# A transformer block on one core: relu chunks transposed out of the banks, their transfers on one queue, relu and square in one instruction

## The chip, the cores and the metric

The kernel runs on one core of a Trainium2 chip. The core has five engines with a queue of instructions each: TensorE (PE, matmuls into the banks of PSUM), VectorE (DVE), ScalarE (ACT), GpSimd (POOL) and SyncE (SP); DMA transfers are issued from the queue of an engine and run on 16 DMA engines. Each queue runs in order, and engines wait for each other by semaphores. The metric is the device time of one execution in microseconds, a median over runs.

## The reference

One layer (DEPTH = 1) of a decoder trunk over 256 tokens of width 2048, in float32. A conditioning vector gives shifts, scales and gates; then come a token mixer and a channel mixer, each with a normalisation before and after. What the change touches is the channel mixer and the gates' rows:

```python
mod = (c_act @ w_ada[l] + b_ada[l]).reshape(b, N_MOD, 1, d)
shift1, scale1, gate1, shift2, scale2, gate2 = [mod[:, i] for i in range(N_MOD)]
h = rms_norm(x, norm_g[l, 0]) * (1.0 + scale1) + shift1
y = token_mixer(h, ...)                      # pooling, gMLP and sparse attention, gated and merged
x = x + gate1 * rms_norm(y, norm_g[l, 1])
h = rms_norm(x, norm_g[l, 2]) * (1.0 + scale2) + shift2
f = jnp.square(jax.nn.relu(h @ w_ff1[l])) @ w_ff2[l]       # 2048 -> 8192 -> 2048
x = x + gate2 * rms_norm(f, norm_g[l, 3])
```

## The kernel before, in words

Tokens are two tiles of 128 (NT = 2), the width 16 tiles of 128 channels (KT = 16). Every large product goes through `gemm` (512 output columns, all 256 tokens): a weight tile of 128 x 2048 (four channel tiles, 1 MB) is loaded into one of three tiles named `raw`, and `split` turns half of it at a time into a hi part on ScalarE (`whi`, L175) and a lo part on VectorE (`wlo`, L176), in three buffers each. `mm_a` then makes three matmuls per channel tile and token tile (hi x hi, lo x hi, hi x lo; L188 to L190), so that a `gemm` is 8 splits and 96 matmuls. A split unit is 12 matmuls. The splits have a raised priority, and a scheduler that follows priorities sets the final order of each queue.

The feed-forward part runs in four passes (`qt`). A pass has four chunks (`m`) of 512 hidden columns: `gemm` of w_ff1, relu of the two banks on ScalarE (L953), and `to_channels`, which turns the chunk from tokens to channels on the partitions. VectorE transposes 32 x 32 blocks (L934), 16 DMAs of 32 KB each move the blocks to their partitions (`moved<-tr`, L938; eight from SyncE, eight from GpSimd), ScalarE squares (L942), and `hi_lo` makes the chunk's hi part (`fhi`, ScalarE, L396) and lo part (`flo`, VectorE, L397). Then four `gemm` of w_ff2 read the pass's 16 channel tiles of fhi and flo, the last chunk's tiles in the last two split units of the first of them.

Beside the products, `fill` steps side work once for every weight tile. In the feed-forward part it is `ada_gate`: 16 loads of 1 MB into `raw` tiles with a reduction each on VectorE (L263), which give the second gate as columns, and then `to_rows` (L290 to L299), which turns the gate's 16 columns to rows with a TensorE transpose, copies them to a `raw` tile, and sends them through DRAM to all partitions as `gg`. `to_rows` also runs once for the first gate, between the products of the token mixer. All loads of `raw` tiles go from SyncE's queue.

## Time and profile before

| | us |
|---|---|
| median of 3 runs (lowest, highest) | 1487.23 (1486.66, 1489.45) |
| the profiled execution, its own time | 1489.17 |
| its span, first to last instruction | 1487.4 |
| TensorE busy | 1417.6 (95%) |
| VectorE busy | 1049.2 (71%) |
| ScalarE busy | 813.1 (55%) |
| GpSimd busy | 94.6 (6%) |

The profile is of one execution. A busy time is the union of an engine's instructions; matmuls overlap each other, so that one which takes 0.39 us starts some 0.23 us after the one before. In the timelines, the bracket at the end of a row is how long the engine stood idle before it, and what ended that. The mean granted clock of TensorE over the span is 0.994 of full speed.

### The profile page before, as it was taken

How to read it: one execution, taken by the hardware profiler on the slowest of the kernel's cores; microseconds unless marked ns; L12 is line 12 of the kernel's file. 1: busy time of each engine (PE TensorE's matmuls, PEld its weight loads, DVE VectorE, ACT ScalarE, POOL GpSimd, SP SyncE). 2: the span in 40 equal slices, each digit the busy share in tenths (PEclk: the TensorE clock that was granted, in tenths of full speed). 3: DMA queues.
4: the chain of work that ended last, by engine and by line, in shares of the span. 5: the costliest groups of instructions: out<-in, count | busy, mean ns of one | idle time of the engine just before them, and what ended most of it. 6: DMA issues, size and time to landing. Idle time of an engine off the chain costs nothing.

```text
span 1487.4 us, 17515 instructions
## 1 busy us (share of the span) xinstructions
PE 1417.6 (95%) x6362; PEld 1155.3 (78%) x6362; DVE 1049.2 (71%) x1315; ACT 813.1 (55%) x1184; POOL 94.6 (6%) x165
## 2 busy tenths in 40 slices
PE   3989999899999999999999999999999999999997
PEld 2777787788777777778778888888887788887886
DVE  6988887668988886788786666566655555554555
ACT  4566666864677873444475543355434453344542
POOL 0000001002010010000001210022001120011100
PEclk9999999999999999999999999999999999999999
DMA  8989788657667568888855776677764765555653
GB/s 315 386 329 368 298 330 307 219 175 255 230 227 285 196 243 319 313 309 302 320 199 184 260 271 239 234 267 269 248 242 172 271 221 190 190 208 190 221 198 113
DMA packets 64695, 376.02 MB, mean 253 GB/s; under 512 B 10288, under 2 KB 14560, under 8 KB 24160
## 3 DMA queue, kind: packets, MB, share of 16 engines
q1 hardware_dynamic: 58848, 364.35, 67.9%
q0 software_dynamic: 5760, 10.55, 2.3%
q8 instruction: 50, 0.82, 0.2%
q14 instruction: 37, 0.30, 0.1%
HBM read 364.35 MB, written 2.11 MB: 246 GB/s over the span
## 4 chain that ended last, share of the span: by engine, by line
PE 79%; DVE 9%; DMA 6%; ACT 3%; issue 2%; SPq 0%; POOL 0%; DVEq 0%; ACTq 0%
PE ps_mm L189 25%; PE ps_mm L190 25%; PE ps_mm L188 24%; DVE wlo L176 4%; DMA raw<-in_w_adaT_dram 3%; DVE raw L263 2%; ACT whi L175 1%; DMA raw<-in_win_g_dram 1%; PE ps_x L666 1%; DMA x_h<-in_x_dram 1%; DMA raw<-in_w_br_nsa_dram 1%; PE ps_pv L658 1%; PE ps_pv L530 0%; DMA raw<-in_w_out_dram 0%; PE ps_pv L657 0%
## 5 line engine op out<-in xcount | busy, mean ns | idle before, releaser
L176 DVE TENSOR_TENSOR wlo<-raw,whi 128x1024 fp32r<-128x1024 f32 x479 | 571.9, 1205 | 321.0 <-ACT whi L175 319.5
L175 ACT ACTIVATE whi<-raw 128x1024 fp32r<-128x1024 f32 x479 | 492.5, 1035 | 493.5 <-PE ps_mm L190 391.3
L189 PE MATMUL ps_mm<-wlo,hhi 128*128 128x512 f32 x1240 | 491.3, 396 | 14.3 <-DVE wlo L176 14.3
L188 PE MATMUL ps_mm<-whi,hhi 128*128 128x512 f32 x1240 | 485.3, 395 | 11.3 <-ACT whi L175 7.6
L190 PE MATMUL ps_mm<-whi,hlo 128*128 128x512 f32 x1240 | 486.9, 393 | 0.0
L189 PEld LDWEIGHTS ps_mm<-wlo,hhi 128*128 128x128 f32 x1240 | 235.2, 190 | 72.1 <-DVE wlo L176 24.9
L188 PEld LDWEIGHTS ps_mm<-whi,hhi 128*128 128x128 f32 x1240 | 234.8, 190 | 62.5 <-ACT whi L175 10.3
L190 PEld LDWEIGHTS ps_mm<-whi,hlo 128*128 128x128 f32 x1240 | 234.5, 189 | 47.8 <-DVE hlo L316 0.4
L263 DVE CUSTOM_DVE_ANT_0 raw<-raw,sil 128x2048 f32<-128x2048 f32 x96 | 220.0, 2293 | 11.6 <-DMA raw<-in_w_adaT_dram 11.4
L189 PE MATMUL ps_mm<-wlo,fhi 128*128 128x512 f32 x496 | 193.2, 390 | 0.0
L188 PE MATMUL ps_mm<-whi,fhi 128*128 128x512 f32 x496 | 193.2, 390 | 0.0
L190 PE MATMUL ps_mm<-whi,flo 128*128 128x512 f32 x496 | 193.2, 390 | 0.0
L938 POOL DMA_DIRECT2D moved<-tr x128 | 62.6, 497 | 739.3 <-DVE tr L934 560.4
L190 PEld LDWEIGHTS ps_mm<-whi,flo 128*128 128x128 f32 x496 | 93.2, 188 | 19.3
L189 PEld LDWEIGHTS ps_mm<-wlo,fhi 128*128 128x128 f32 x496 | 93.2, 188 | 19.2
L188 PEld LDWEIGHTS ps_mm<-whi,fhi 128*128 128x128 f32 x496 | 93.2, 188 | 19.2
L397 DVE TENSOR_TENSOR flo<-r32c,fhi 128x512 fp32r<-128x512 f32 x32 | 20.7, 688 | 24.1 <-ACT fhi L396 24.1
L393 ACT ACTIVATE ps_mm<-part 128x512 f32<-128x512 f32 x40 | 23.5, 597 | 11.5 <-DVE part L382 7.0
L639 ACT ACTIVATE e<-e,m 128x128 f32<-128x128 f32 (+1 forms) x64 | 28.2, 443 | 0.7 <-DVE m L636 0.6
L942 ACT ACTIVATE r32c<-moved 128x512 f32<-128x512 f32 x32 | 18.4, 622 | 16.0 <-DMA moved<-tr 15.4
L953 ACT ACTIVATE r_t<-ps_mm 128x512 f32<-128x512 f32 x32 | 18.8, 588 | 14.7 <-PE ps_mm L190 14.7
L189 PE MATMUL ps_mm<-wlo,qe 128*128 128x512 f32 x64 | 25.3, 395 | 1.3 <-DVE wlo L176 1.3
(284 smaller groups left out, 1103.8 us busy)
## 6 DMA issues: line engine op xcount, KB each, us to landing
raw<-in_w_ff_dram SPq DMA_DIRECT2D x128, 1024.0 KB, 5.0
raw<-in_w_adaT_dram SPq DMA_DIRECT2D x96, 1024.0 KB, 6.2
raw<-in_win_g_dram SPq DMA_DIRECT2D x32, 1024.0 KB, 5.1
raw<-in_win_e_dram SPq DMA_DIRECT2D x24, 1024.0 KB, 5.3
raw<-in_win_e_dram SPq DMA_DIRECT2D x24, 768.0 KB, 6.3
raw<-in_w_out_dram SPq DMA_DIRECT2D x16, 1024.0 KB, 6.3
raw<-in_w_br_nsa_dram SPq DMA_DIRECT2D x8, 1024.0 KB, 5.2
raw<-in_win_e_dram SPq DMA_DIRECT2D x12, 512.0 KB, 6.0
```

The lines of the kernel that those rows point to most:

```text
L175: A.activation(hv, v, AF.Copy)
L176: V.tensor_sub(lv, v, hv.bitcast(F32))
L188: T.matmul(outs[t], ahi[:, kt, ts_], hv[:, k, c0:c0 + n], start=f, stop=False, skip_group_check=True)
L189: T.matmul(outs[t], ahi[:, kt, ts_], lv[:, k, c0:c0 + n], start=False, stop=False, skip_group_check=True)
L190: T.matmul(outs[t], alo[:, kt, ts_], hv[:, k, c0:c0 + n], start=False, stop=l, skip_group_check=True)
L263: V.tensor_tensor_reduce(raw, raw, sil, 0.5, 0.0, ALU.mult, ALU.add, accum_out=col)
L393: A.activation(ps, early[e][0][:, b * 512:(b + 1) * 512], AF.Copy)
L397: V.tensor_sub(lo, src, hi.bitcast(F32))
L639: A.activation(e[:, br, 0:L], e[:, br, 0:L], AF.Exp, scale=-1.0, bias=m8[:, hh, br:br + 1], accum_out=s8[:, hh, br:br + 1])
L938: (nc.sync if j % 2 else G).dma_start(moved[32 * j:32 * j + 32, q].rearrange("p t m i -> p (t m i)"), tr[32 * q:32 * q + 32, j].rearrange( ...
L942: A.activation(r32[:, :, t * P:(t + 1) * P].rearrange("p m (q i) -> p m q i", i=32), moved[:, :, t].rearrange("p q m i -> p m q i"), AF.Sq ...
L953: A.activation(r_t[:, t], ps[t], AF.Relu)
```

## The change

In `to_rows` the gate's rows are copied into the first 16 partitions of the constant tile's triangle (`triu`, last read by the gMLP mixer), and no `raw` tile is taken. In the feed-forward part the relu on ScalarE goes: VectorE transposes straight from the two banks, all 16 DMAs of a chunk are issued from GpSimd, and one VectorE instruction on the moved tile takes max(x, 0) * x in place. The hi and lo parts are then made by token tile (t) instead of by pairs of channel tiles, and read the moved tile in the order of the channels.

```diff
-        gr = st.tile([P, 2048], F32, name="raw", tag="raw", bufs=3)[0:KT, 0:P]
+        gr = triu[0:KT]
         V.tensor_copy(gr, tb[0:KT, 0:P])
         row = dp.tile([KT, P], F32, name="row", tag="row", bufs=2)
         G.dma_start(row, gr)
...
-    def to_channels(m, r_t):
+    def to_channels(m, ps):
         tr = fl.tile([P, 4, NT, 4, 32], F32, name="tr")
         for t in range(NT):
-            V.transpose(tr[:, :, t], r_t[:, t].rearrange("p (m j i) -> p j m i", m=4, j=4))
-        moved = fl.tile([P, 4, NT, 4, 32], F32, name="moved", tag="moved", bufs=1)
+            V.transpose(tr[:, :, t], ps[t].rearrange("p (m j i) -> p j m i", m=4, j=4))
+        moved = fl.tile([P, 4, NT, 4, 32], F32, name="moved")
         for q in range(4):
             for j in range(4):
-                (nc.sync if j % 2 else G).dma_start(moved[32 * j:32 * j + 32, q].rearrange("p t m i -> p (t m i)"),
-                                                    tr[32 * q:32 * q + 32, j].rearrange("p t m i -> p (t m i)"))
-        r32 = fl.tile([P, 4, S], F32, name="r32c", tag="r32c", bufs=1)
+                G.dma_start(moved[32 * j:32 * j + 32, q].rearrange("p t m i -> p (t m i)"),
+                            tr[32 * q:32 * q + 32, j].rearrange("p t m i -> p (t m i)"))
+        mf = moved.rearrange("p q t m i -> p (q t m i)")
+        V.scalar_tensor_tensor(mf, mf, 0.0, mf, ALU.max, ALU.mult)
         for t in range(NT):
-            A.activation(r32[:, :, t * P:(t + 1) * P].rearrange("p m (q i) -> p m q i", i=32),
-                         moved[:, :, t].rearrange("p q m i -> p m q i"), AF.Square)
-        for k in range(2):
-            s = slice(4 * m + 2 * k, 4 * m + 2 * k + 2)
-            hi_lo(flat(fhi[:, s]), flat(flo[:, s]), flat(r32[:, 2 * k:2 * k + 2]))
+            ts_ = slice(t * P, (t + 1) * P)
+            hv, lv = (f[:, 4 * m:4 * m + 4, ts_].rearrange("p m (q i) -> p m q i", i=32) for f in (fhi, flo))
+            hi_lo(hv, lv, moved[:, :, t].rearrange("p q m i -> p m q i"))
...
             ps = gemm(ff1_v, qt * 4 + m, act) if qt or m else ps_first
-            r_t = fl.tile([P, NT, 512], F32, name="r_t", tag="r_t", bufs=2)
-            for t in range(NT):
-                A.activation(r_t[:, t], ps[t], AF.Relu)
-            to_channels(m, r_t)
+            to_channels(m, ps)
```

The scheduler also puts other instructions in another order. VectorE's queue in the last pass, one chunk before the change (tr is the transposed chunk, wlo the lo part of a weight split, flo the chunk's lo part):

```order
L934 STREAM_TRANSPOSE tr<-r_t 128x4x128
L176 TENSOR_TENSOR wlo<-raw,whi 128x1024
L934 STREAM_TRANSPOSE tr<-r_t 128x4x128
L176 TENSOR_TENSOR wlo<-raw,whi 128x1024 x3
L397 TENSOR_TENSOR flo<-r32c,fhi 128x512 x2
L176 TENSOR_TENSOR wlo<-raw,whi 128x1024 x4
```

And the same chunk now:

```order
L934 STREAM_TRANSPOSE tr<-ps_mm 128x4x128 x2
L176 TENSOR_TENSOR wlo<-raw,whi 128x1024 x4
L941 SCALAR_TENSOR_TENSOR moved<-moved 128x1024
L176 TENSOR_TENSOR wlo<-raw,whi 128x1024
L397 TENSOR_TENSOR flo<-moved,fhi 128x4x128 x2
L176 TENSOR_TENSOR wlo<-raw,whi 128x1024 x3
```

The two transposes stand together, and the new instruction stands behind four lo parts, with one more between it and the chunk's own lo part.

ScalarE's queue before, at the first two chunks of the third pass (r_t is the relu's output, r32c the square's, fhi the chunk's hi part):

```order
L953 ACTIVATE r_t<-ps_mm 128x512
L175 ACTIVATE whi<-raw 128x1024
L953 ACTIVATE r_t<-ps_mm 128x512
L175 ACTIVATE whi<-raw 128x1024
L942 ACTIVATE r32c<-moved 128x4x128 x2
L396 ACTIVATE fhi<-r32c 128x512 x2
L175 ACTIVATE whi<-raw 128x1024 x6
L953 ACTIVATE r_t<-ps_mm 128x512
L175 ACTIVATE whi<-raw 128x1024
L953 ACTIVATE r_t<-ps_mm 128x512
L175 ACTIVATE whi<-raw 128x1024 x3
L942 ACTIVATE r32c<-moved 128x4x128 x2
```

And now, in the same place:

```order
L396 ACTIVATE fhi<-moved 128x4x128 x2
L175 ACTIVATE whi<-raw 128x1024 x8
L396 ACTIVATE fhi<-moved 128x4x128 x2
L175 ACTIVATE whi<-raw 128x1024 x8
L396 ACTIVATE fhi<-moved 128x4x128 x2
```

Relus and squares are gone, and eight hi parts of weights stand between the hi parts of one chunk and the next.

SyncE's queue before at the first gate's rows, in the token mixer (adaT are the loads of the side work, x_ the tile of the residual):

```order
L843 DMA x_5631<-in_x_dram 128x2048
L165 DMA raw<-in_w_br_nsa_dram 128x2048
L262 DMA raw<-in_w_adaT_dram 128x2048
L843 DMA x_5631<-in_x_dram 128x2048
L165 DMA raw<-in_w_br_nsa_dram 128x2048
L262 DMA raw<-in_w_adaT_dram 128x2048
L165 DMA raw<-in_w_br_nsa_dram 128x2048
L262 DMA raw<-in_w_adaT_dram 128x2048
L165 DMA raw<-in_win_g_dram 128x2048 x2
```

And now:

```order
L843 DMA x_5630<-in_x_dram 128x2048
L165 DMA raw<-in_w_br_nsa_dram 128x2048
L262 DMA raw<-in_w_adaT_dram 128x2048
L165 DMA raw<-in_w_br_nsa_dram 128x2048
L262 DMA raw<-in_w_adaT_dram 128x2048
L165 DMA raw<-in_w_br_nsa_dram 128x2048
L262 DMA raw<-in_w_adaT_dram 128x2048
L843 DMA x_5630<-in_x_dram 128x2048
L165 DMA raw<-in_win_g_dram 128x2048 x2
```

The second load of x stands four loads later than before, behind the loads that surround the gate's rows. In the feed-forward part SyncE's queue keeps the loads alone.

## Rows read from the trace of the kernel before

**Rows 1.** The page, busy time of each engine.
```profile
PE 1417.6 (95%) x6362; PEld 1155.3 (78%) x6362; DVE 1049.2 (71%) x1315; ACT 813.1 (55%) x1184; POOL 94.6 (6%) x165
```
**Rows 2.** Stretches: length, busy time (instructions) by engine, clock, DMA share, GB/s.
```profile
785.00:1150.00 365.00, 365.00 (x1612) 302.48 (x1611) 225.94 (x219) 168.46 (x185) 35.19 (x72) 1.00 0.69 241
...
1050.00:1100.00 50.00, 50.00 (x222) 41.43 (x221) 31.06 (x29) 19.12 (x19) 0.00 (x0) 1.00 0.68 242
1150.00:1200.00 50.00, 46.70 (x193) 37.61 (x192) 26.11 (x26) 25.07 (x30) 8.89 (x18) 0.93 0.72 252
...
1350.00:1400.00 50.00, 47.68 (x203) 38.77 (x202) 25.92 (x25) 23.63 (x30) 9.78 (x20) 0.97 0.59 194
```
**Rows 3.** Timeline of TensorE at 1155 us: start, duration, instruction, idle before.
```profile
1155.00 1.22 PE L188 MATMUL ps_mm<-whi,hhi 128*128 128x512 f32 x2 [3.27 <-ACT whi L175]
...
1157.28 0.63 PE L189 MATMUL ps_mm<-wlo,hhi 128*128 128x512 f32 x1
```
**Rows 4.** The chain that ended last, at 1143 to 1149 us.
```profile
1143.75 0.51 SPq L938
...
1148.81 4.98 DMA raw<-in_w_ff_dram
```
**Rows 5.** Waits of SyncE's queue: total us, times, longest us.
```profile
SPq L938 <- DVE tr L934: 45.2, 16, 13.6
...
SPq L165 <- DMA row<-raw: 12.7, 2, 6.6
```
**Rows 6.** Timeline of ScalarE at both stalls.
```profile
1150.40 1.15 ACT L942 ACTIVATE r32c<-moved 128x512 f32<-128x512 f32 x2 [5.84 <-DMA moved<-tr]
1151.59 1.15 ACT L396 ACTIVATE fhi<-r32c 128x512 fp32r<-128x512 f32 x2
1153.89 2.00 ACT L175 ACTIVATE whi<-raw 128x1024 fp32r<-128x1024 f32 x2 [1.16 <-DMA raw<-in_w_ff_dram]
...
1358.07 1.15 ACT L942 ACTIVATE r32c<-moved 128x512 f32<-128x512 f32 x2 [5.29 <-DMA moved<-tr]
```
**Rows 7.** Timeline of GpSimd, an undisturbed chunk and the one of 1347 us.
```profile
1194.46 3.90 POOL L938 DMA_DIRECT2D moved<-tr  x8 [17.83 <-DVE tr L934]
...
1351.46 1.96 POOL L938 DMA_DIRECT2D moved<-tr  x4 [2.72 <-issue]
```
**Rows 8.** Timeline of VectorE in the undisturbed chunk.
```profile
1191.18 0.71 DVE L934 STREAM_TRANSPOSE tr<-r_t 128x512 f32<-128x512 f32 x1 [0.35 <-ACT r_t L953]
...
1195.04 1.23 DVE L176 TENSOR_TENSOR wlo<-raw,whi 128x1024 fp32r<-128x1024 f32 x1 [0.87 <-ACT whi L175]
...
1200.48 1.23 DVE L176 TENSOR_TENSOR wlo<-raw,whi 128x1024 fp32r<-128x1024 f32 x1 [1.49 <-ACT whi L175]
```
**Rows 9.** Timeline of ScalarE in the undisturbed chunk.
```profile
1190.55 0.60 ACT L953 ACTIVATE r_t<-ps_mm 128x512 f32<-128x512 f32 x1 [0.98 <-PE ps_mm L190]
1191.23 1.06 ACT L175 ACTIVATE whi<-raw 128x1024 fp32r<-128x1024 f32 x1
```
**Rows 10.** Transfers to moved: chunk of 1194 us, chunk of 1347, chunks to 1100.
```profile
DMA to landing us min/median/max: 1.7/1.8/2.2
...
DMA to landing us min/median/max: 1.7/1.9/4.9
...
DMA to landing us min/median/max: 1.8/3.4/5.0
```
**Rows 11.** Two lines of VectorE: durations ns min/median/max, first and last start, forms.
```profile
L142 DVE SCALAR_TENSOR_TENSOR sil<-xnT,sil x2: 1225/1226/1226, 5.8 to 7.3; 128x1024 f32<-128x1024 f32 x2
...
L966 DVE COPY fsum<-ps_mm x8: 680/682/684, 879.2 to 945.1; 128x512 f32<-128x512 f32 x8
```
**Rows 12.** The first gate's rows: SyncE, TensorE, and the stretch around.
```profile
585.92 0.33 SPq L165 DMA_DIRECT2D raw<-in_w_br_nsa_dram  x1
...
584.68 1.38 PE L343 MATMUL ps_x<-cst,mab 128*128 128x128 f32 x8 [1.55 <-DVE mab L815]
...
575.00:600.00 25.00, 21.49 (x95) 16.21 (x93) 17.48 (x22) 6.60 (x7) 1.11 (x2) 1.00 0.78 305
```

## The prediction

> **What bounds the kernel now.** I read the page's busy shares first, then the busy time by stretch of 50 us, then the chain that ended last, and last the timelines of the engines round the two stretches that stood out. The page shows TensorE busy 1417.6 us, 95% of the span [rows 1], so whatever the change does to other engines counts only through TensorE's gaps and its clock. The stretches show where these are in the feed-forward part, which runs from about 785 us to the end: from 785 to 1150 us TensorE is busy 365.00 of 365.00 us at the full clock, and a clean stretch holds 222 matmuls in 50 us, one per 0.2252 us [rows 2]. So in the first eight of the sixteen chunks the relus, squares and transfers that the change touches lie wholly under TensorE, and nothing is gained by taking them off. Two stretches are not clean: 1150 to 1200 us holds 193 matmuls, 29 fewer, and 1350 to 1400 us holds 203, 19 fewer [rows 2]. These are all that the feed-forward part can give back before its tail: 29 x 0.2252 = 6.5 us (stall A) and 19 x 0.2252 = 4.3 us (stall B). Of A 3.3 us are idle time (46.70 us busy of 50), of B 2.3; the rest, 3.2 and 2.0, is slow clock.
>
> Stall A: TensorE waits 3.27 us for a hi part and then runs on with matmuls that take 0.63 us [rows 3]; the granted clock of that 50 us is 0.93 of full [rows 2], so for some 7 us it was at the lower of its two levels (1.2 GHz), right after the idle time. The chain goes back through the load of the weight tile, issued at 1148.81 when SyncE had its eight transfers out, the first at 1143.75 [rows 4]; SyncE had been standing at these transfers until the second transpose was done (16 such waits, 13.6 us the longest), and two of its loads waited for the gate rows' transfer to let a raw tile go (6.6 us the longest) [rows 5]. A second cause lies beside it: ScalarE stood 5.84 us before the first square, with the next hi parts behind it in its queue [rows 6]; without the late load the next hi part could have started at 1151.59 + 1.15 = 1152.7 instead of 1153.89, which is 1.2 us of the 3.3. Stall B is this second cause alone: ScalarE stands 5.29 us before the square [rows 6], because GpSimd's eight transfers came in two groups of four with 2.72 us between them for which the profile has no reason [rows 7], and some of them took up to 4.9 us to land where 1.9 was the middle [rows 10].
>
> **The change part by part.** For each chunk I take the one at 1191 us, undisturbed and without the gate's reduction, as model, and walk through it with the new order. The chunk's last matmul ends at about 1191.2, when the first hi part behind it starts [rows 9]; call that T.
>
> Relus: 32 x 0.6 us leave ScalarE, and the first transpose no longer waits for one. The transposes read the banks. A copy of 128x512 out of a bank takes VectorE 0.682 us, and a transpose from a tile 0.71 [rows 8, 11]; no row shows a transpose from a bank, so it lies between 0.68 and, if the two simply added, 1.39 us. I take 0.71, since the copy shows that a bank feeds VectorE at the rate that the transpose needs. VectorE was free at 1191.18 and the first bank was done by 1190.55, when its relu began [rows 8, 9]; both transposes stand side by side in the new order, so they end by 1192.6, 1.9 us before GpSimd's first issue of now.
>
> Transfers: eight on GpSimd take 3.90 us, 0.49 each [rows 7], and begin within 0.3 us of the second transpose's end. Sixteen in one row begin at 1192.9, the last is issued at 1192.9 + 15 x 0.49 = 1200.2 and lands 1.8 us later [rows 10] at 1202.0. From GpSimd's ninth on, each waits for one eight before it, issued 3.9 us earlier; that costs nothing at 1.8 us and up to 1.1 us at the 5.0 us that loads beside it make of it at worst [rows 10].
>
> Relu and square in one: 128x1024 on VectorE. The nearest row is the same operation on the same size, 1.226 us [rows 11]. It cannot be less than that row; if relu and square cost an instruction each it would be 2.45, which would take 1.2 us of the room below. I take 1.23. The hi parts read the moved tile in the pattern in which the squares read it, 1.15 us for two [rows 6]; for the lo parts, which read it so for the first time, I take the 0.65 of a half that a lo part's 1.23 gives, and at most twice that. It stands behind four lo parts in VectorE's order, of which the last ends at 1201.7 [rows 8]. This is the wait that the change adds: the four squares' wait on ScalarE goes, and instead VectorE stands at this instruction until the last transfer has landed, with the next lo part, the chunk's two lo parts and through them TensorE behind it. In the model it runs from 1202.0 to 1203.3. The next lo part ends at 1204.5, the first half of the chunk's lo (0.65 us) at 1205.2, the second at 1205.8. TensorE has two split units (12 matmuls, 2.70 us each) ahead of the one whose lo part stands there: it needs it 72 matmuls after T, at 1191.2 + 16.2 = 1207.4. For the last chunk of each four, the same moment is when the second product first reads the chunk, and its lo only two matmuls later, at 1207.9. The tightest of them, the first lo half, is 2.7 us early. So in the model chunk nothing waits; 16 x 1.23 us of VectorE and the loss of ScalarE's 32 x 0.6 both lie under TensorE.
>
> At the Trainium skill's warning I looked hardest here. The row shows eight issues in 3.90 us with a lo part running beside them [rows 7, 8]. The Trainium skill, "SBUF — State Buffer", section "SBUF: two separate sides", says that transfers issued from GpSimd starve while VectorE runs instructions that take both of its port pairs, and advises another queue. By this rule the sixteen issues could each wait for an instruction of VectorE; by the row they do not wait for a subtraction, and the reduction and the in-place product are not shown beside them. That is the second rival below.
>
> SyncE: 128 issues go, about 5 us a chunk (1143.75 to 1148.81) [rows 4], and with them its standing at the transposes. Weight loads then go out as raw tiles come free. Together with the raw tile that the gate rows no longer hold, this removes the late load of stall A; the new order of ScalarE removes its other cause, because there are eight splits from one chunk's hi parts to the next one's all through, where the chunk of stall A had its squares one split behind the second relu. So A goes wholly: -6.5, or a third of it, -2.4, if only the load's part went (1.2 of 3.3 us). Stall B goes if GpSimd's gap does not come again: -4.3, and 0 if it does.
>
> Gate rows, first use: the load at 585.92 went out when the raw tile came free, and TensorE waited 1.55 us for a sum before its transposes [rows 12]. Without the tile that load can go out up to 6 us earlier, and its splits and matmuls stand ahead of the transposes in the new order. Against this, 1 MB of x moves behind the next reduction's load, in among the gate rows' broadcast and the next weight loads. What the earlier load takes out of this crowd, x puts back, so the weight tile that ends the gap comes at about the same time. I take 0. The bounds: -3.5 if all of TensorE's idle time from 575 to 600 us goes (25 - 21.49), +3.4 if 1 MB simply comes on top at the 305 GB/s of that stretch [rows 12].
>
> The sum, on the profiled execution: 1489.17 us (span 1487.4 and 1.8 around it) - 6.5 - 4.3 + 0 = 1478.4. The median shown is 1487.23, 1.9 lower. If the other runs held both stalls in full the median becomes 1476.4; if the 1.9 is a part of the stalls that they lacked, it becomes 1478.4. I take the middle, 1477.5.
>
> **The rivals.** First, late transfers: a gap such as the one before stall B comes again, now with 256 issues on one queue where 128 had it once. For it: GpSimd is exposed for 7.8 us a chunk instead of 3.9, and the profile names no cause. A gap of 2.72 and landings of 4.9 instead of 1.8 make 5.8 us, 3.1 more than the model's room, so about 3 us idle and, as in B, 2.0 us of slow clock: 1482.5 with one such chunk, 1487.5 with two. Against it: one gap in 128 issues is all there is.
>
> Second, and slower than before: GpSimd's issues stretch because VectorE's instructions hold them up. That room of 2.7 us is gone at 0.49 + 2.7/15 = 0.67 us an issue; that is the point from which it decides. At 1.0 us the last lands 7.7 us later, TensorE idles 5.0 us in each chunk and loses as much to the clock as B, 2.0: 16 x 7.0 = 112, so about 1590. Against it stands the even 0.49 in row after row; for it, that VectorE's reduction, in seven chunks, now falls among the sixteen.
>
> Third, the gate rows' stretch moves on its own by its bounds, with the rest as forecast: 1474 or 1481.
>
> Fourth, the change does not do all that it says: stall A stays in part, since TensorE there only needs something to be late, and the chunk after the gate rows has the copy, the lo parts and the product close together on VectorE. Half of A back is 1481; all of it 1484.
>
> **How the numbers follow.** Forecast 0.62 (1474.5 to 1480), late transfers 0.17, slow issues 0.04, the gate rows' stretch 0.09, stall A in part 0.08. The time is that of the forecast, 1477.5. The range of 8 in 10 goes from 1473.0 (gate rows at their better bound) to 1484.5 (one late chunk, or most of A); two late chunks and slow issues are left out. This kernel's measurements tell 0.2%, 3 us, from no change: faster is all of the forecast and of the third, most of the late transfers and half of the fourth, 0.86; the same 0.10; slower 0.04.
>
> **What would show it.** Right: no gap of TensorE between 785 us and the tail, 222 matmuls in each 50 us; GpSimd's sixteen issues in 7.8 us; the in-place product starting within a microsecond of the last landing and ending before the next lo part is due; no wait of SyncE for a transpose. Wrong: issues of 0.67 us or more; matmuls of 0.63 us behind a wait for a lo part that stands behind the in-place product; a transpose from a bank over 1.4 us; a gap of over 2.7 us near 595 us where there were only smaller ones.

## The result: 1.2% slower, and the profile after

| | before | after |
|---|---|---|
| median of 6 runs each (lowest, highest), us | 1487.64 (1483.58, 1489.55) | 1502.37 (1498.54, 1507.37) |
| ratio after / before, 95% interval | | 1.0118 [1.0097, 1.0140] |
| profiled execution, its own time / span, us | 1489.17 / 1487.4 | 1502.06 / 1500.3 |

The forecast was 1477.5 us, 1473.0 to 1484.5. The time lies outside the range, on the other side of no change.

The page of the kernel after, the row that answers to [rows 1]:

```profile
PE 1422.4 (95%) x6362; PEld 1157.8 (77%) x6362; DVE 1063.1 (71%) x1331; ACT 777.4 (52%) x1120; POOL 157.2 (10%) x293
```

TensorE's busy share is the same to the per cent; ScalarE lost 36 us and GpSimd gained 63. Only the stretches show where the time went. The three that answer to [rows 2], same columns (length, then PE, PEld, DVE, ACT and POOL, then clock, DMA share, GB/s):

```profile
785.00:1150.00 365.00, 349.86 (x1510) 285.83 (x1509) 222.35 (x214) 141.83 (x143) 62.63 (x128) 0.99 0.68 236
...
1150.00:1200.00 50.00, 48.18 (x213) 39.43 (x213) 28.20 (x29) 20.18 (x22) 16.73 (x34) 1.00 0.64 212
1350.00:1400.00 50.00, 46.38 (x202) 38.03 (x201) 27.29 (x28) 19.89 (x21) 15.64 (x32) 0.99 0.57 190
```

The first stretch, which was full before, now holds 1510 matmuls instead of 1612: 102 x 0.2252 = 23.0 us are lost there. The two stretches that were to come clean hold 213 and 202 of 222, another 6.5 us. What TensorE waited for, over the whole span (total us, times, longest us; before the change the first of these waits took 16.6 us in all, 1.5 the longest, and the second did not occur):

```profile
PE ps_mm L189 <- DVE wlo L176: 28.5, 19, 3.6
...
PE ps_mm L188 <- ACT fhi L396: 3.6, 2, 2.1
```

The first row are waits for lo parts, which VectorE makes; 16.7 of its 28.5 us lie in the feed-forward part. The second are waits for the chunk's own hi part, in the last chunks of the first two passes. Together that is 20.3 us. The two old stalls have indeed left their places; nine of the sixteen chunks have a gap of over a microsecond instead. One of them, the second chunk of the first pass, in full. Its second transpose ends at 812.8. First GpSimd's transfers and SyncE's loads (four of them from 811.61 on, one at 815.02, 2.2 us after the transpose), then VectorE, ScalarE and TensorE in time order:

```profile
813.35 5.86 POOL L938 DMA_DIRECT2D moved<-tr  x12 [13.72 <-ACT whi L175]
820.90 2.05 POOL L938 DMA_DIRECT2D moved<-tr  x4 [1.70 <-DMA moved<-tr]
...
811.61 11.22 SPq L165 DMA_DIRECT2D raw<-in_w_ff_dram  x4
```
```profile
812.73 2.25 DVE L263 CUSTOM_DVE_ANT_0 raw<-raw,sil 128x2048 f32<-128x2048 f32 x1
...
821.25 1.23 DVE L176 TENSOR_TENSOR wlo<-raw,whi 128x1024 fp32r<-128x1024 f32 x1 [1.50 <-ACT whi L175]
827.85 1.23 DVE L941 SCALAR_TENSOR_TENSOR moved<-moved 128x1024 f32<-128x1024 f32 x1 [5.37 <-DMA moved<-tr]
828.99 1.22 DVE L176 TENSOR_TENSOR wlo<-raw,whi 128x1024 fp32r<-128x1024 f32 x1
```
```profile
829.11 1.15 ACT L396 ACTIVATE fhi<-moved 128x512 fp32r<-128x512 f32 x2 [5.17 <-DVE moved L941]
```
```profile
830.26 0.50 PE L189 MATMUL ps_mm<-wlo,hhi 128*128 128x512 f32 x1 [1.75 <-DVE wlo L176]
```

Read from the bottom: TensorE stands 1.75 us for the lo part that started at 828.99; that stood behind the in-place product, and the product stood 5.37 us for transfers. The chain that ended last goes through the same place (start, us, what):

```profile
813.35 1.95 POOL moved L938 x4
815.29 5.33 DMA moved<-tr
...
820.90 1.47 POOL moved L938 x3
822.45 5.31 DMA moved<-tr
...
828.99 1.23 DVE wlo L176
830.26 0.50 PE ps_mm L189
```

Two landings stand one behind the other: the twelfth issue is out, GpSimd waits for a transfer eight back, and only then issues the last four, of which the sixteenth takes 5.3 us again. The landings of this chunk, and below them those of the first chunk of the third pass, which has no side load (us, min/median/max; [rows 10] has those of before):

```profile
DMA to landing us min/median/max: 2.8/5.1/6.8
```
```profile
DMA to landing us min/median/max: 1.7/3.4/5.2
```

In that third-pass chunk the sixteen go out as forecast, and the product waits 1.53 us and holds nobody up:

```profile
1158.62 3.91 POOL L938 DMA_DIRECT2D moved<-tr  x8 [101.41 <-ACT whi L175]
1162.75 3.91 POOL L938 DMA_DIRECT2D moved<-tr  x8 [0.21 <-issue]
```
```profile
1169.27 1.23 DVE L941 SCALAR_TENSOR_TENSOR moved<-moved 128x1024 f32<-128x1024 f32 x1 [1.53 <-DMA moved<-tr]
```

Its last transfer lands 11.1 us after the second transpose, where the model of the prediction had 1202.0 - 1192.6 = 9.4. The trace shows what the landings go by. A weight load that was on its way at the transpose lands 4.2 us after it, and the first eight transfers land right behind it, at 4.4 to 5.6 us. The next load is issued at 4.2 us, between the eighth transfer and the ninth, and lands at 9.6; the last eight land right behind that one, at 9.9 to 11.1.

In the first eight chunks the last transfer lands after 13.3 to 16.4 us; before the change it was 6.2 to 7.6. With 13.3 us TensorE still had no gap, with 14.7 it had 2.33 us: between these two lies the room that this order of VectorE's queue leaves to the transfers.

### The profile page after: what moved, and what is told of

The parts are those of the page before. It is cut to its first block, busy times and chain, and to the rows that moved or that the text cites. A ratio compares the mean times of both kernels' runs of the same rounds, so it can differ in the third digit from the quotient of the medians.

```text
span 1500.3 us, 17227 instructions
## 1 busy us (share of the span) xinstructions
PE 1422.4 (95%) x6362; PEld 1157.8 (77%) x6362; DVE 1063.1 (71%) x1331; ACT 777.4 (52%) x1120; POOL 157.2 (10%) x293
## 4 chain that ended last, share of the span: by engine, by line
PE 73%; DMA 10%; DVE 8%; ACT 3%; issue 3%; POOL 2%; SPq 0%; DVEq 0%; ACTq 0%
PE ps_mm L189 23%; PE ps_mm L190 23%; PE ps_mm L188 22%; DMA moved<-tr 7%; DVE wlo L176 4%; POOL moved L938 2%; ACT whi L175 1%; DVE raw L263 1%; DMA raw<-in_w_out_dram 1%; PE ps_x L666 1%; DMA x_h<-in_x_dram 1%; DMA raw<-in_win_g_dram 1%; PE ps_pv L658 1%; PE ps_pv L530 0%; PE ps_pv L657 0%
## 5 line engine op out<-in xcount | busy, mean ns | idle before, releaser
L189 PE MATMUL ps_mm<-wlo,hhi 128*128 128x512 f32 x1240 | 492.1, 397 | 27.7 <-DVE wlo L176 27.4
L938 POOL DMA_DIRECT2D moved<-tr x256 | 125.2, 497 | 686.3 <-ACT whi L175 465.2
L941 DVE SCALAR_TENSOR_TENSOR moved<-moved 128x1024 f32<-128x1024 f32 x16 | 19.6, 1225 | 68.2 <-DMA moved<-tr 68.2
L396 ACT ACTIVATE fhi<-moved 128x512 fp32r<-128x512 f32 x32 | 18.4, 623 | 65.0 <-DVE moved L941 65.0
L382 DVE COPY part<-ps_mm 128x512 f32<-128x512 f32 x28 | 19.2, 686 | 10.0 <-PE ps_mm L190 10.0
L188 PE MATMUL ps_mm<-whi,qe 128*128 128x512 f32 x64 | 25.2, 394 | 0.0
```

The costliest lines, as they stand in the source:

```text
L188: T.matmul(outs[t], ahi[:, kt, ts_], hv[:, k, c0:c0 + n], start=f, stop=False, skip_group_check=True)
L189: T.matmul(outs[t], ahi[:, kt, ts_], lv[:, k, c0:c0 + n], start=False, stop=False, skip_group_check=True)
L382: V.tensor_copy(d, ps)
L396: A.activation(hi, src, AF.Copy)
L938: G.dma_start(moved[32 * j:32 * j + 32, q].rearrange("p t m i -> p (t m i)"), tr[32 * q:32 * q + 32, j].rearrange("p t m i -> p (t m i)"))
L941: V.scalar_tensor_tensor(mf, mf, 0.0, mf, ALU.max, ALU.mult)
```

## The experiments

All times are medians; the ratio is against the kernel before, run beside them on the same chip (its medians there: 1487.64 for the first row, 1484.62 for experiments 1 to 4, 1485.16 for 5 to 8, 1482.86 for 9 and 10). "FF" is the feed-forward part: from the end of the first chunk's second transpose to the end of the span, in one profile each. It is 691.8 us before the change and 712.6 after. Where the first chunk starts differs between profiles of kernels with the same code ahead of it (by 12 us between the first and the fifth experiment), so only FF is compared profile by profile. The last two columns give how long after the second transpose the last transfer landed, in chunks 1 to 8 (those with side loads) and 9 to 16.

| kernel | median | ratio [95%] | FF | landing 1-8 | 9-16 |
|---|---|---|---|---|---|
| after | 1502.37 | 1.0118 [1.0097, 1.0140] | 712.6 | 13.3-16.4 | 11.0-16.6 |
| 1 two queues | 1473.40 | 0.9929 [0.9903, 0.9954] | 683.5 | 7.0-8.0 | 7.3-11.3 |
| 2 gate rows alone | 1475.37 | 0.9939 [0.9915, 0.9962] | 685.4 | 6.2-8.1 | 6.2-11.7 |
| 3 one queue alone | 1540.13 | 1.0387 [1.0336, 1.0438] | 744.4 | 12.3-17.2 | 11.2-15.7 |
| 4 no side loads | 1485.76 | 1.0019 [0.9994, 1.0045] | 695.1 | 11.1-16.3 | 10.9-16.8 |
| 5 ten memsets | 1473.08 | 0.9914 [0.9889, 0.9939] | 683.3 | 6.8-8.3 | 7.2-11.3 |
| 6 product later | 1483.18 | 0.9994 [0.9966, 1.0022] | 692.1 | 14.6-16.3 | 10.9-16.9 |
| 7 GpSimd and ScalarE | 1496.13 | 1.0064 [1.0033, 1.0095] | 703.8 | 9.9-12.7 | 7.1-12.3 |
| 8 SyncE alone | 1490.92 | 1.0039 [1.0012, 1.0066] | 697.7 | 11.3-11.8 | 11.3-13.3 |
| 9 six and ten | 1471.10 | 0.9911 [0.9888, 0.9935] | 681.9 | 7.5-8.2 | 7.5-8.4 |
| 10 gate rows, six and ten | 1480.37 | 0.9979 [0.9958, 0.9999] | 688.0 | 7.5-8.7 | 7.5-8.7 |

The theory was that the one queue is the whole loss: it makes the transfers late, and by no longer holding SyncE's loads back it lets these run beside them. The rivals were the new wait on VectorE as such and the transposes out of the banks. In each experiment the scheduler ordered the queues anew, so an edit can move more than it names; where that bears on the reading, the text says so.

**1. Two queues.** The changed kernel, transfers from both queues again.

```diff
-                G.dma_start(moved[32 * j:32 * j + 32, q]...
+                (nc.sync if j % 2 else G).dma_start(moved[32 * j:32 * j + 32, q]...
```

> The changed kernel with one edit undone: the sixteen transfers of a chunk go again from SyncE and GpSimd in turn. Theory (loads beside the transfers): SyncE's eight transfers had kept the 1 MB weight loads out until they were issued, so the last one lands 6 to 8 us after the second transpose instead of 11 to 16.6; VectorE then finds the moved tile landed when it comes to the in-place product, and TensorE has no gap from 785 us to the tail. The changed kernel's feed-forward part takes 718.6 us from its first transpose to the end of the span, against 699.2 before, of which the two stalls were 10.8, so 30 us go: about 1472. Rival (the wait on VectorE): what costs is that the relu and square stand in VectorE's queue, whatever the transfers do; then the time stays at 1495 to 1502. Rival (transposes from the banks): the same, 1495 to 1502.

29.1 us of FF come back with this one edit, and 1473.4 us is where the theory had it. The transposes from the banks and the product on VectorE are still there, so both rivals fall. (The scheduler also moved the product: from the second chunk on it stands behind three lo parts of weights instead of four, which leaves the transfers less room, not more.) The second chunk of the first pass, SyncE:

```profile
815.40 0.33 SPq L165 DMA_DIRECT2D raw<-in_w_ff_dram  x1
816.63 4.97 SPq L938 DMA_DIRECT2D moved<-tr  x8
821.71 6.14 SPq L165 DMA_DIRECT2D raw<-in_w_ff_dram  x3
```

No load goes out while the transfers are issued; the product waits 1.6 us. FF is also 8.3 us shorter than before the change: most of the 10.8 that were forecast for the two stalls.

**2. Gate rows alone.** The kernel before with one line changed.

```diff
-        gr = st.tile([P, 2048], F32, name="raw", tag="raw", bufs=3)[0:KT, 0:P]
+        gr = triu[0:KT]
```

> The kernel before with only the gate rows' copy moved out of the raw tiles. Between the first gate's transpose and the first transposed chunk the changed kernel gained 8.6 us (582.9 to 788.2 us before, 585.0 to 781.7 now). If the raw tile is what held that stretch back, this kernel gains the same 8 us there, and at least the late load's part of stall A: 1475 to 1479. If the gain comes from the other edits' shifts in the schedule, or is chance, 1487.

0.6% faster, at the better edge of what was expected: 9.3 of the 11.2 us by which experiment 1 is under the kernel before, run beside it. Its stretches say from where (stall A's, stall B's, and the first gate's rows):

```profile
1150.00:1200.00 50.00, 50.00 (x222) 41.37 (x222) 28.92 (x30) 26.86 (x32) 8.93 (x18) 1.00 0.70 242
1350.00:1400.00 50.00, 47.33 (x201) 38.45 (x200) 28.43 (x28) 27.79 (x35) 7.84 (x16) 0.97 0.57 196
```
```profile
575.00:600.00 25.00, 24.09 (x111) 19.41 (x110) 21.25 (x26) 9.04 (x10) 1.11 (x2) 1.00 0.89 343
```

Stall A is gone, with SyncE's eight transfers and with relus and squares still on ScalarE. But the order moved with the line. In the chunk of stall A ScalarE had one weight split between the second relu and the squares before the change, and stood 5.84 us at the squares [rows 6]; now it has three, as in the pass's other chunks, and stands 0.22:

```profile
1139.55 0.58 ACT L953 ACTIVATE r_t<-ps_mm 128x512 f32<-128x512 f32 x1
1141.30 1.06 ACT L175 ACTIVATE whi<-raw 128x1024 fp32r<-128x1024 f32 x1 [1.17 <-PE ps_mm L190]
1144.02 1.06 ACT L175 ACTIVATE whi<-raw 128x1024 fp32r<-128x1024 f32 x1 [1.66 <-PE ps_mm L190]
1146.74 1.06 ACT L175 ACTIVATE whi<-raw 128x1024 fp32r<-128x1024 f32 x1 [1.66 <-PE ps_mm L190]
1148.02 1.15 ACT L942 ACTIVATE r32c<-moved 128x512 f32<-128x512 f32 x2 [0.22 <-DMA moved<-tr]
```

So this one line takes away both of the causes that the prediction gave for A, and what each was worth stays open. Stall B stays (201 matmuls, [rows 2] has 203). And the first gate's rows gain 111 - 95 = 16 matmuls against [rows 12], 3.6 us; the kernel after has the same 111. (The same 25 us do not hold quite the same work in each profile. The 100 matmuls of large products that follow the 1900th take 27.4 us before and in experiment 3, which keeps the raw tile, and 22.8 or 22.9 in the ten kernels without it.)

**3. One queue alone.** The kernel before with all sixteen transfers on GpSimd; the gate rows keep their raw tile.

```diff
-                (nc.sync if j % 2 else G).dma_start(moved[32 * j:32 * j + 32, q]...
+                G.dma_start(moved[32 * j:32 * j + 32, q]...
```

> The kernel before with all sixteen transfers of a chunk issued from GpSimd; relus and squares stay on ScalarE. Theory (loads beside the transfers): the last transfer lands 11 to 16 us after the second transpose, ScalarE stands at the square with the next hi parts behind it, and TensorE idles in most of the first eight chunks: 1500 to 1515. Rival (the wait on VectorE): ScalarE bears the wait as it did before, 1487.

Slower than was expected (1500 to 1515): FF is 52.6 us longer than before. Here ScalarE stands at the squares with the next hi parts behind it, and these are late sooner than VectorE's product is in the changed kernel (ScalarE, then TensorE, at 1024 us):

```profile
1023.47 1.15 ACT L942 ACTIVATE r32c<-moved 128x512 f32<-128x512 f32 x2 [7.96 <-DMA moved<-tr]
```
```profile
1026.79 0.50 PE L188 MATMUL ps_mm<-whi,hhi 128*128 128x512 f32 x1 [4.22 <-ACT whi L175]
```

So the move of the wait from ScalarE to VectorE helps the late transfers; it does not cause the loss.

**4. No side loads.** The changed kernel with 15 of the 16 side loads of the feed-forward part left out (one tile is loaded and reduced again and again; the second gate's values are not computed).

```diff
+    def ada_gate_once():
+        raw = fl.tile([P, 2048], F32, name="adaraw")
+        nc.sync.dma_start(raw, w_adaT[5 * D:5 * D + P, :])
...
-    side["ada"][0] += [ada_gate(5, V_BG2, V_G3, g2_col), to_rows(g2_col, gg2)]
+    side["ada"][0] += [ada_gate_once(), to_rows(g2_col, gg2)]
```

> The changed kernel without fifteen of the sixteen 1 MB side loads of the second gate in the feed-forward part (one tile is loaded once and reduced sixteen times, so the second gate's values are left wrong; work and order of the rest as in the changed kernel). Theory (loads beside the transfers): with one load less among a chunk's transfers, the first eight chunks land about 11 us after the second transpose as six of the later eight do, and lose their gaps, some 13 us of idle time and 6 of slow clock: about 1483. Rival (one queue by itself is too slow): they land at 14 to 16 us as now, and the time stays at 1495 to 1502.

17.5 of the 29.1 us go with the side loads, near what was expected. (The loads that go out among the transfers are weight tiles of the products; what the side loads decide is when. In the second chunk they go out 2.2, 4.5 and 9.7 us after the transpose in the changed kernel, and here at 4.5 and 11.2. The sixteen reductions also move, all into the first pass.) What is left is mostly two chunks whose landings are at 16.3 and 16.8 us; GpSimd stands in the middle of both, in front of the 111th and the 230th transfer. The first:

```profile
1009.12 2.94 POOL L948 DMA_DIRECT2D moved<-tr  x6 [0.22 <-issue]
1014.67 0.50 POOL L948 DMA_DIRECT2D moved<-tr  x1 [2.61 <-issue]
```

The changed kernel stands at the same two transfers (4.52 us and 2.66 us), and [rows 7] show the same before, in front of the 109th. The next experiment asks what it goes by.

**5. Ten memsets.** Experiment 1 with ten memsets on GpSimd ahead of the first chunk.

```diff
+    idle = fl.tile([P, 10], F32, name="idle")
+    for i in range(10):
+        G.memset(idle[:, i:i + 1], 0.0)
```

> The kernel with the change but two queues (SyncE and GpSimd) for the transfers, and ten small GpSimd instructions of no use ahead of the first chunk. In every run so far GpSimd stands about 2.7 us with no releaser in front of one certain transfer: the 109th of 128 on its queue before the change, the 111th and the 230th of 256 after it. Theory (the stand belongs to a place in GpSimd's queue): ten instructions more move it ahead of the chunk's first transfer, where GpSimd stands anyway; the chunk at about 1340 us lands its last transfer 7.5 us after the second transpose instead of 11.3, TensorE's 1.05 us gap behind it goes, and the time is 1.4 us under the two-queue kernel's 1473.4: 1472. Rival (it belongs to the moment, or to the traffic of that chunk): the gap stays in the chunk of 1340 us, 1473.4.

The theory of this experiment falls: the stand is in front of the 109th transfer again, and the chunk lands at 11.3 us as without the memsets.

```profile
1327.48 1.96 POOL L941 DMA_DIRECT2D moved<-tr  x4 [17.86 <-ACT whi L175]
1332.15 1.96 POOL L941 DMA_DIRECT2D moved<-tr  x4 [2.71 <-issue]
```

So it goes neither by the count of instructions nor by the moment (1341 us in experiment 1, 1027 us in the changed kernel). In every kernel so far it came when GpSimd had issued 128 DMAs; experiment 9 tries that.

**6. Product later.** The changed kernel, but in the first three chunks of a pass the in-place product is held back behind the last weight split of the next product.

```diff
+            if u == 12 and chunks:
+                with tc.issue_after(last_lo[0].ins):
+                    chunks.pop(0)()
...
+        if m < 3:
+            chunks.append(finish)
+        else:
+            finish()
```

> The changed kernel, all transfers on GpSimd, but in the first three chunks of each pass the in-place product stands behind six lo parts of weights on VectorE instead of four, 5.4 us of TensorE's work later. Theory (late landings reach TensorE only because VectorE stands at the product with the next lo parts behind it): the landings stay as late as they are, but the seven gaps of TensorE behind such chunks (16.7 of the 20.3 us idle) go and those of the last chunks of the first two passes (3.6 us) stay; 30 us x 16.7/20.3 = 25 us less than 1502.4: 1474 to 1482. Rival (the transfers slow the weight loads, and TensorE waits for weights): 1497 to 1504.

The landings are as late as in the changed kernel (14.6 to 16.3 us), and yet 20.5 us of FF come back: a little less than was expected, 1483.2 us instead of 1474 to 1482. VectorE in the second chunk:

```profile
825.66 1.23 DVE L178 TENSOR_TENSOR wlo<-raw,whi 128x1024 fp32r<-128x1024 f32 x1 [1.50 <-ACT whi L177]
826.86 1.23 DVE L947 SCALAR_TENSOR_TENSOR moved<-moved 128x1024 f32<-128x1024 f32 x1
```

In this chunk the product no longer waits. TensorE's gaps that are left are in the last chunks of three passes (1.44, 2.77 and 1.98 us), where the chunk itself is needed. So late landings reach TensorE through VectorE standing at the product, and not through slow weight loads, which was the rival.

**7. GpSimd and ScalarE.** The changed kernel, half of the transfers from ScalarE: two queues, SyncE's loads not held back.

```diff
+                (nc.scalar if j % 2 else G).dma_start(moved[32 * j:32 * j + 32, q]...
```

> The changed kernel with half of the transfers issued from ScalarE instead of GpSimd, so that there are two queues but SyncE's loads are not held back. Theory A (the second queue is what helps: eight issues take 4 us instead of 8 and no transfer waits for an earlier one): transfers take 3 to 5 us beside the loads, the last lands 8 to 9.5 us after the second transpose, inside the room of about 13; no gaps, 1473 to 1479. Theory B (the loads that SyncE's transfers held back are what hurts): landings over 13 us in the first eight chunks again, 1490 to 1502.

Neither theory as it stood: the time is where theory B had it, but the landings of chunks 2 to 8 are at 11.0 to 12.7 us, between the two. GpSimd's eight issues take 3.9 us; ScalarE's eight are out 5.4 us after the second transpose, in two groups of four with a hi part of a weight between them. The loads that go out 2.2 us and 5.0 us after the second transpose stretch what is on its way (second chunk):

```profile
DMA to landing us min/median/max: 3.5/5.3/7.9
```

The first chunk of the third pass shows it on a single transfer. Fifteen of its sixteen take 3.5 to 5.0 us and have landed 7.7 us after the second transpose. The sixteenth is issued at 1159.7, 0.8 us behind the fifteenth and 0.1 us behind a weight load. The load lands 10.0 us after the transpose, and the sixteenth transfer at 10.4, 2.8 us after the fifteenth (the load, then the sixteenth alone):

```profile
1159.61 0.33 SPq L165 DMA_DIRECT2D raw<-in_w_ff_dram  x1
```
```profile
DMA to landing us min/median/max: 5.4/5.4/5.4
```

TensorE loses time at these landings (9 gaps, up to 2.56 us) because VectorE's order here has the product behind three lo parts of weights instead of four; with the changed kernel's order 13.3 us cost nothing. Its time is therefore no measure of the transfers, the landings are.

**8. SyncE alone.** The changed kernel, all sixteen on SyncE: one queue, the loads stand behind it.

```diff
+                nc.sync.dma_start(moved[32 * j:32 * j + 32, q]...
```

> The changed kernel with all sixteen transfers on SyncE: one queue, but weight loads stand behind it. Theory A (one queue is what hurts): the ninth waits for the first as on GpSimd, landings 13 us and more after the second transpose, 1495 to 1505. Theory B (loads beside the transfers are what hurts): 16 x 0.59 = 9.4 us of issues, each landing about 2 us after its issue since no load goes out among them, the last at 11.4 in all chunks, inside the room; but the loads that went out 5 us after the transposes now go out at 9.5, and what TensorE waits for then is a hi part whose load is late: 1474 to 1490.

The landings and the waits are as theory B had them; the time, 1490.9, is just past the end of its range. SyncE, and the landings of the second chunk:

```profile
812.77 10.55 SPq L938 DMA_DIRECT2D moved<-tr  x16
823.42 1.48 SPq L165 DMA_DIRECT2D raw<-in_w_ff_dram  x3
```
```profile
DMA to landing us min/median/max: 1.8/2.3/3.9
```

One queue with no load issued among its transfers lands the last at 11.3 to 11.8 us in all of the first eight chunks, inside the room. What TensorE waits for now is the other thing that was expected, the hi part of a weight tile whose load came late:

```profile
829.61 0.73 PE L188 MATMUL ps_mm<-whi,hhi 128*128 128x512 f32 x2 [1.46 <-ACT whi L175]
830.87 0.50 PE L189 MATMUL ps_mm<-wlo,hhi 128*128 128x512 f32 x1 [0.53 <-DVE wlo L176]
```

Experiments 1, 7 and 8 and the changed kernel are a square; the second chunk's landing is 7.9 us with two queues and loads held back, 11.8 with one queue and loads held back, 12.7 with two queues and loads free, 15.0 with one queue and loads free. One queue costs 3.9 or 2.3 us, free loads 4.8 or 3.2, and only both together pass the room of 13.3 to 14.7. The issuing engines differ between the corners (SyncE alone takes 10.0 to 10.6 us for its sixteen issues, GpSimd 7.8 where it does not wait), so these parts are rough.

**9. Six and ten.** Experiment 1 with six transfers on GpSimd and ten on SyncE.

```diff
-                (nc.sync if j % 2 else G).dma_start(moved[32 * j:32 * j + 32, q]...
+                (nc.sync if j % 2 or q == 3 else G).dma_start(moved[32 * j:32 * j + 32, q]...
```

> The changed kernel with two queues again, six transfers of a chunk on GpSimd and ten on SyncE. In the kernels so far GpSimd stood about 2.7 us after it had issued 128 DMAs in all: 18 ahead of the first chunk, 108 transfers and the gate's two rows before the change (in front of the 109th transfer), 18 and 110 after it (in front of the 111th); ten memsets did not move it. Theory (the stand goes by the number of DMAs issued on this queue): with 18 + 96 + 2 = 116 it never comes, all sixteen chunks land within 6.5 to 9 us after the second transpose, TensorE has no gap from 785 us to the tail, and the six matmuls lost at 1350 us in the two-queue kernel come back: 1473.2 - 1.4 = 1471.8. Rival (the stand belongs to the time or the traffic of that chunk): it comes again at about 1340 us. Second rival: ten issues on SyncE (5.9 us) hold the loads too long and TensorE waits for hi parts, as with all sixteen there: 1475 to 1485.

GpSimd does not stand; the chunk that landed at 11.3 us lands at 8.4. From 785 us to the tail TensorE has no gap at all:

```profile
785.00:1460.00 675.00, 675.00 (x2980) 558.95 (x2979) 417.17 (x408) 283.36 (x295) 48.06 (x98) 1.00 0.65 227
```

This kernel has the lowest median and the shortest FF, 0.9% under before. That it is 2.3 us under experiment 1 is inside what the medians tell apart, and its ratio is that of experiment 5; FF, 1.6 us shorter than in experiment 1, is as expected.

**10. Gate rows, six and ten.** Experiment 2 with the same six and ten; relus and squares on ScalarE.

> The kernel before with the gate rows in the constant tile alone (relus and squares on ScalarE), six transfers on GpSimd and ten on SyncE. With the stand gone, 21 matmuls that were lost at 1350 us come back, 4.7 us of 1475.4: 1470.7. If the straight transposes and the one-instruction relu and square are worth anything by themselves, this is slower than the same transfers with them (1471.8 expected); the theory says that all of it lies under TensorE, and both are within 2 us of each other. Rival (ScalarE, with relus and squares in front of its hi parts, is still late somewhere): a gap of TensorE for a hi part is left, 1473 to 1478.

The theory's part on relu and square falls. Stall B goes, but new gaps come in chunks with side loads, and the median is 9.3 us over that of experiment 9 with the same transfers (FF 6.1 us), past the rival's range too. TensorE, and ScalarE's hi part that it waited for through VectorE:

```profile
859.22 0.50 PE L189 MATMUL ps_mm<-wlo,fhi 128*128 128x512 f32 x1 [2.31 <-DVE wlo L176]
```
```profile
858.32 1.06 ACT L175 ACTIVATE whi<-raw 128x1024 fp32r<-128x1024 f32 x1 [3.25 <-DMA raw<-in_w_ff_dram]
```

A late load stands ahead of the hi part. In the same chunks of experiment 9 loads are held as long (6.4 to 7.0 us) and TensorE waits for none; what makes the difference, the relus and squares between ScalarE's splits or the order that the scheduler gave the loads with them, was not separated. With eight and eight (experiments 1 and 2) the two forms differ by 1.9 us of FF.

## Why the prediction was wrong, point by point

**Transfers: the step that failed.** "the last is issued at 1192.9 + 15 x 0.49 = 1200.2 and lands 1.8 us later": this took a landing time from a chunk in which SyncE's queue was held by its own eight transfers and no side load ran, and used it for all sixteen chunks. The issues came as forecast (0.49 us each); the landings were 3.9 us in the median and 7.3 at most over all 256. Even in the chunk without a side load the last one took 3.0 us, because a weight load was issued between the eighth transfer and the ninth, and the last eight landed only behind it. The prediction had the number that decides: 5.0 us at worst in the chunks to 1100 us [rows 10], and up to 1.1 us for the ninth's wait. 9.4 + 1.1 + (5.0 - 1.8) = 13.7 us, against a room that ended at 9.4 + 2.7 = 12.1. That bound lay past the room in the chunks where it was measured; it was named, and then kept for a rival with one or two late chunks. For eight chunks, 1.6 us idle and the 2.0 of slow clock that it took from stall B make 29 us, the size of the loss, but part of that agreement is luck: nine chunks had a gap, 2.3 us each in the mean, and of the 29.5 us of matmuls that the stretches lost only about 9 are not idle time, 1.0 a gap. The wait for a transfer eight back came in eight chunks and was sized low as well: 1.1 to 2.2 us.

**SyncE: an edit counted as a gain only.** "Weight loads then go out as raw tiles come free" was right and was the harm. SyncE's eight transfers had been holding the loads back for 5 us, just while the transfers were on their way. Freed, a load went out 2.2 us after the second transpose and another at 4.5 us (second chunk). Experiments 1, 7 and 8 show it, in that chunk: 3 to 5 us of landing from the freed loads, 2 to 4 us from the one queue. The two belong together: sixteen issues in one row take 7.8 us, and the later an issue, the likelier a new load stands ahead of it. Experiment 7's sixteenth transfer shows what that costs, 2.8 us for 0.8 us of delay.

The Trainium skill, "DMA: Bandwidth & Descriptors", section "Issuing engines are not separate DMA queues", says that transfers from several issuing engines share the same DMA engines, and that a second issuer only saves the usually small issuing time. The first half agrees with experiment 7, where two issuing engines left the landings at up to 7.9 us beside SyncE's loads. Of the second half, that only issuing time is saved fits too: sixteen issues take 7.8 us on one queue and eight take 3.9, and the one queue cost 2.3 and 3.9 us of landing. That it is small does not hold here: it is 4 us of a room of 13.

**The wait that the change adds** was placed rightly: VectorE at the product, the next lo part behind it, TensorE behind that. So were the size of the product (1.23 us, measured 1.226) and of a transpose from a bank (0.71, measured 0.671 to 0.717 over 32). The room was read a little short: 12.1 us after the second transpose, and TensorE had no gap at 13.3.

**Stalls A and B** went where the landings allowed it. Experiment 9 has both full, 50.00 us busy of 50, and its FF is 9.9 us shorter than before, against -6.5 - 4.3 = -10.8. Of A's two causes, experiment 2 takes away both with the raw tile alone, since ScalarE's order changes with it; "So A goes wholly" came true, and the split of 1.2 us and 2.1 between the two causes was not tested.

**Stall B's cause** "for which the profile has no reason" was GpSimd's stand, and it came again in every kernel that issued as many DMAs on GpSimd. The first rival was right in kind: 256 issues met it twice, in chunks 7 and 15, as against once for 128. It added to late landings that were there without it.

**Gate rows, first use,** "I take 0": measured -3.6 us (16 matmuls in the stretch; -4.5 over the same 100 matmuls), at the better bound of -3.5 or past it. "What the earlier load takes out of this crowd, x puts back" did not happen: the loads moved 342 GB/s in that stretch instead of 305 [rows 12].

**Slow issues,** the second rival, fell: twelve issues in 5.86 us, 0.488 each, with the reduction of 812.73 on VectorE beside them. By the Trainium skill's rule in "SBUF — State Buffer", section "SBUF: two separate sides", they might have waited; no row of these runs shows it, with the reduction, the subtraction or the transposes.

**The sum.** FF +20.8 us in the profiles, the gate rows -3.6: +17.2. The medians say +14.7. The remaining 2.5 us are less than the runs of either kernel spread over (6 and 9 us). The two profiled spans differ by 12.9 us only: besides the gate rows, some 4 us were saved ahead of the feed-forward part, and that part of the span differs by as much between kernels that have the same code there.

## What to carry to other kernels

A transfer's landing time belongs to what runs beside it: when an edit takes instructions off a queue, ask what that queue issues next, and what is then still unissued behind it. Use the worst landing of the stretches that have such neighbours, in the sum and not in a rival. If that bound passes the room, the forecast is a stall. And a wait costs by what stands behind it on its engine: two lo parts more ahead of the product were worth 20 us with every transfer as late as before.

## What the runs showed of the hardware

In all nine kernels that issued more than 128 DMAs on GpSimd's queue, it stood 2.6 to 2.8 us (4.52 in one), with no releaser in the profile, when 128 had been issued: 18 ahead of the first chunk, then 108 transfers and the gate's two rows before the change and in experiments 1, 2, 5 and 7, or 110 transfers with one queue (the changed kernel and experiments 3, 4 and 6). In these four a second stand came in front of the 230th transfer, 121 DMAs on. Ten memsets did not move it, and with 116 DMAs in all (experiment 9) it did not come. What it is, the profile does not say, nor whether it goes by the number of DMAs or by what they carry. In the changed kernel's chunk 7 it fell on late landings and took 4.52 us.

A 32 KB transfer took 1.9 us from issue to landing in the median where SyncE issued it with no load among its transfers (experiment 8), and up to 7.9 us beside two loads of 1 MB (experiment 7). Over all twelve kernels, 2459 of the 3072 transfers were issued with one or more 1 MB loads on their way; all but six landed after the first of those loads had (the six up to 1.4 us before it). In the changed kernel these are 253 of 256, all but one.
